# Splitting the first weights of a phase early, taking POOL out of the phase change and fixing ScalarE's order, in a fp32 two-layer decoder trunk on one Trainium2 core

## The chip, the core and the metric

One core of one Trainium2 chip runs the whole program. The engines are TensorE (PE, with its weight loads PEld), VectorE (DVE), ScalarE (ACT), GpSimd (POOL) and SyncE (SP, which here issues nearly all DMAs). The time is device microseconds of one execution; lower is better. Before: 2397.88 us, the median of 3 runs (2392.67 to 2399.52).

## What is computed

A trunk of two layers over 256 tokens and 2048 channels. Layer 0 mixes tokens by a Conformer convolution, layer 1 by differential attention; each is followed by a squared-ReLU MLP of 8192 hidden channels. Scales, shifts and gates come from a condition vector `c` by a product with `ada_w` (six vectors in each layer). Cut to what matters here:

```python
cond = silu(c)
for i in range(2):
    sh_m, sc_m, g_m, sh_f, sc_f, g_f = split(cond @ ada_w[i] + ada_b[i], 6)
    h = x * (1 + sc_m) + sh_m
    y = conformer_conv(h, ...) if i == 0 else diff_attention(h, ...)   # ends in a 2048x2048 projection
    x = layer_norm(alpha * x + g_m * y, ln_mix_g[i], ln_mix_b[i])
    h = x * (1 + sc_f) + sh_f
    y = square(relu(h @ mlp_w1[i] + mlp_b1[i])) @ mlp_w2[i] + mlp_b2[i]
    x = layer_norm(alpha * x + g_f * y, ln_ffn_g[i], ln_ffn_b[i])
```

## The kernel before

**Products.** Every matrix is float32 and is split into a high part (rounded to the fp32r type) and a low part (the rest). A product is the sum of three: high by high, high by low, low by high. `x`-side pairs such as `hT` lie as (channel in chunk, chunk, token); weights stream from DRAM in tiles of 128 x 2048 (four chunks of 128 rows by 512 columns), four raw buffers deep, and are split in halves of 128 x 1024: ACT casts the high half (`wh_...`), DVE or POOL subtracts to get the low half (`wl_...`). There are four buffers for split halves (pool `wsp`). A half serves two chunks, two token halves and three products: 12 products.

**Jobs.** `add_group` cuts a product of 512 output columns into jobs. A normal job is one raw tile, two halves, with both token halves (t = 0, 1) done for each weight half. The last job of a phase (`tail`) and the first of the next (`lead`) hold four halves and run all of them for t = 0 and then for t = 1, so that the layer norm and the next h of t = 0 can be made while t = 1 is multiplied. `run_jobs` writes the program: `fetch(n)` emits load, cast and subtraction of the weight halves up to number n, `half(j, t)` the products, `tick()` releases work that was put off by a number of ticks (a normal job makes two, one for each 12 products). `POOL_LEAD` names the lead halves whose low part POOL makes, `POOL_TAIL` those of the tail.

**Phase change.** There are three: convolution to first MLP (some 485 us into the span), first MLP to attention (1233 us), attention to second MLP (1644 us). At each, the chain for one token half is: gate and add to `z` (L724, L725), statistics (L1152 or L1262, L642, L647), a power on POOL (L120), `nb` (L653), normalise `z` in four quarters, two on ACT (L660) and two on DVE (L662); TensorE transposes four blocks (L453); scale and shift give h (L458 on ACT for blocks 0 and 2, L461 on DVE for blocks 1 and 3), whose high part ACT casts (L411) and whose low part DVE subtracts (L414; POOL for block 3). The scalars for scale and shift come from `h_scalars` (L737 to L740 on DVE). `z` is then multiplied on POOL by the layer norm's gain, for the next residual (`base_x`, L695 to L699, four quarters, each with its own small load on SP), first after 6 ticks, then every 4 or 5.

**Order.** From the first job on, TensorE and DVE run in the order in which the code is written; ACT, POOL and SP run in an order that a scheduler chose when the program was built.

Of the kernel before, what the change touches and what calls it, by code (L numbers as in the profile page):

```python
# [19 lines left out]
P = 128  # L20
# [22 lines left out]
AHEAD = 4  # L43
POOL_LO = (3,)
U_WAIT = 2
POOL_LEAD = (1,2,3)
POOL_TAIL = (-1,-3)
GF_LOAD = 16
M2 = (196, 207)
# [30 lines left out]
def trunk(  # L80
# [431 lines left out]
    def add_group(key, pair, srcs, lead=False, tail=False, pump=None, start=None, pre_t=None, on_t=None,  # L512
                  only=None, prep=None, between=None, on_pool=(), bias=None):
        blocks = [[i] for i in range(len(srcs))]
        if lead:
            blocks[:2] = [[0, 1]]
        if tail:
            blocks[-2:] = [[len(srcs) - 2, len(srcs) - 1]]
        per = srcs[0].shape[1]
        for blk in blocks:  # L520
            if only is not None and blk[0] not in only:
                continue
            first = blk[0] == 0
            jobs.append(dict(key=key, pair=pair, n=2 * len(blk), kc0=blk[0] * per, nk=per * len(srcs),
                             start=start if first else None, pre_t=pre_t if first else None, pre_done=False, prep=prep if first else None, on_t=on_t, bias=bias if first else None,
                             between=between if first else None))
            for i in blk:
                for q in range(2):
                    pool = ((lead and 2 * i + q in POOL_LEAD) or (tail and 2 * (i - len(srcs)) + q in POOL_TAIL)
                            or 2 * i + q in on_pool)  # L530
                    halves.append((f"{key}_{i}", srcs[i], q, pump, nc.gpsimd if pool else nc.vector))

    def fetch(n):
        while len(split) < min(n, len(halves)):
            name, src, q, pump, eng = halves[len(split)]
# [4 lines left out]
            hi = wsp.tile([P, 1024], F32R, tag="whi", name=f"wh_{name}_{q}")  # L540
            lo = wsp.tile([P, 1024], F32R, tag="wlo", name=f"wl_{name}_{q}")
            nc.scalar.copy(hi, rq)  # L542
            eng.tensor_tensor(lo, rq, hi.bitcast(F32), op=ALU.subtract)  # L543
            per = src.shape[1] // 2
            hv = hi.rearrange("p (a n) -> p a n", a=per)
            lv = lo.rearrange("p (a n) -> p a n", a=per)
            split.append([(hv[:, a, :], lv[:, a, :]) for a in range(per)])
            if q == 1 and pump is not None:
                pump()

    def run_jobs():
        banks, h = {}, 0
        for n, job in enumerate(jobs):
            if job["start"] is not None:
                job.pop("start")()
                job["start"] = None
            pair = job["pair"]()
            key, nk = job["key"], job["nk"]
            if job["kc0"] == 0:
                banks[key] = [mm_bank(f"{key}_ps{t}") for t in range(NT)]  # L560
            pss = banks[key]

            def half(j, t):

                steps = []
                kc0 = job["kc0"] + j * len(split[h])
                for a, (wh, wl) in enumerate(split[h + j]):
                    kc = kc0 + a
                    for tt in t:
                        if job["pre_t"] is not None and kc == 0 and (tt or not job["pre_done"]):  # L570
                            for f in job["pre_t"](tt):
                                f()
                        xh = pair[0][:, kc, tt * P:(tt + 1) * P]
                        xl = pair[1][:, kc, tt * P:(tt + 1) * P]
                        if kc == 0 and job["bias"] is not None:
                            for n, (sel, row) in enumerate(job["bias"]()):
                                nc.tensor.matmul(pss[tt], lhsT=sel, rhs=row, start=(n == 0), stop=False)
                        nc.tensor.matmul(pss[tt], lhsT=xh, rhs=wh, start=(kc == 0 and job["bias"] is None),  # L578
                                         stop=False)
                        nc.tensor.matmul(pss[tt], lhsT=xh, rhs=wl, start=False, stop=False)  # L580
                        nc.tensor.matmul(pss[tt], lhsT=xl, rhs=wh, start=False, stop=(kc == nk - 1))  # L581
                        if kc == nk - 1 and job["on_t"] is not None:
                            steps.append(lambda tt=tt: job["on_t"](tt, pss[tt]))
                return steps

            if job["n"] == 2:
                for j in range(2):
                    fetch(h + j + AHEAD)
                    for f in half(j, range(NT)):
                        f()  # L590
                    tick()
            else:
                fetch(h + 4)
                tail = []
                for t in range(NT):
                    if job["between"]:
                        job["between"](GF_USE[2 * t])
                    for j in range(4):
                        if job["between"] and j == 2:
                            job["between"](GF_USE[2 * t + 1])  # L600
                        if t == NT - 1:
                            fetch(h + j + AHEAD)
                        steps = half(j, [t])
                        if steps and t == 0:
                            tail = steps[0]() or []
                            nxt = jobs[n + 1] if n + 1 < len(jobs) else None
                            if nxt is not None and nxt["prep"] is not None:
                                tail.append(nxt["prep"])
# [590 lines left out]
    def mlp(i, ln_g, ln_b, gcol, bcol, pump, at_end, start=None, mid=None):  # L1199
# [32 lines left out]
        for q in range(4):  # L1232
            for g in range(4):
                n0 = q * D + g * NG

                def on_t1(t, ps, q=q, g=g, n0=n0):
# [4 lines left out]
                    def rest():  # L1241
                        pt = tp_tile(f"ut_{i}_{q}_{g}_{t}")
                        for j in range(4):
# [10 lines left out]
                add_group(f"w1_{i}_{q}_{g}", lambda: cur["hT"], wtiles(mlp_w1[i], 0, KC, n0), pump=pump, lead=first,  # L1254
                          start=(lambda q=q: begin_q(q)) if g == 0 else None,
                          pre_t=pre_t if first else None, on_t=on_t1, prep=prep if first else None,
                          between=ada_between if first and i == 0 else None)
            for n in range(4):
                def on_t2(t, ps, q=q, n=n):
# [236 lines left out]
    for g in range(4):  # L1496
        kv = {}
        pair = lambda: sc1["hT"]
        add_group(f"qkv_q{g}", pair, wtiles(attn_qkv_w[0], 0, KC, g * NG), pump=pump_slow, lead=(g == 0),
                  start=begin_attn if g == 0 else None, prep=prep_attn if g == 0 else None, pre_t=pre_attn if g == 0 else None,  # L1500
                  on_t=rope_evac("q", g, kv))
        add_group(f"qkv_k{g}", pair, wtiles(attn_qkv_w[0], 0, KC, D + g * NG), pump=pump_slow,
                  on_t=rope_evac("k", g, kv))
# [80 lines left out]
```

## Time and profile before

| | |
|---|---|
| median of 3 runs | 2397.88 us (2392.67 to 2399.52) |
| the profiled execution's own time | 2392.5 us |
| its span | 2390.7 us, 28609 instructions |
| mean granted clock of TensorE | 0.987 |
| TensorE busy | 95% of the span |
| DVE, ACT, POOL busy | 75%, 44%, 10% |
| DMA | 608.54 MB, mean 255 GB/s |

The profile is of one execution. Times in its rows count from the start of the span. A stage row gives the stretch, its length, then for PE, PEld, DVE, ACT and POOL the busy time and (x) the number of instructions, the clock granted to TensorE as a share of full speed, the mean busy share of the DMA engines and GB/s. Matmuls are pipelined, so their durations overlap; what counts is the distance from one start to the next.

### The profile page before, as it was taken

The page shows a single profiled execution, that of the slowest core. Times are in us where ns is not written, and L with a number is a line of the kernel's source. Part 1 is how long each engine was busy: PE and PEld are TensorE (multiplying, and loading weights), DVE is VectorE, ACT ScalarE, POOL GpSimd, SP SyncE. Part 2 cuts the span into 40 slices and gives each one's busy share as a digit, 9 for nine tenths or more (in the row PEclk, how much of TensorE's full clock was granted, in tenths as well). Part 3 has the DMA queues.
Part 4 walks back from the last instruction along what each step waited for, and adds up shares of the span by engine and source line. Part 5 has one row for each costly group of instructions (what it writes and reads, how often), then busy time and mean ns, then how long its engine had stood idle before and what let it go on. Part 6 is the DMA issues. An engine that isn't in the chain of part 4 may idle for free.

```text
span 2390.7 us, 28609 instructions
## 1 busy us (share of the span) xinstructions
PE 2276.4 (95%) x11167; PEld 1814.2 (76%) x11167; DVE 1802.4 (75%) x2046; ACT 1059.9 (44%) x1360; POOL 247.6 (10%) x162
## 2 busy tenths in 40 slices
PE   5899988999899999999989999998999999999997
PEld 3576646777688888888867888876888888888886
DVE  5887887988888889878868777886876565555566
ACT  3433674254334444434444554544443443443442
POOL 0000001130410000000035001013122000000002
PEclk9999999999999999999999999998999999999998
DMA  9998369969898887888856657684876555556562
GB/s 346 343 321 299 139 250 383 347 206 320 312 321 293 318 317 270 324 313 283 306 185 237 221 185 232 233 316 143 294 263 215 187 193 193 179 192 194 188 219 103
DMA packets 271980, 608.54 MB, mean 255 GB/s; under 512 B 11038, under 2 KB 44388, under 8 KB 258532
## 3 DMA queue, kind: packets, MB, share of 16 engines
q1 hardware_dynamic: 271604, 606.41, 73.2%
q8 instruction: 87, 1.43, 0.2%
q10 hardware_dynamic: 240, 0.30, 0.1%
q14 instruction: 49, 0.40, 0.0%
HBM read 604.54 MB, written 2.13 MB: 254 GB/s over the span
## 4 chain that ended last, share of the span: by engine, by line
PE 78%; DVE 12%; DMA 4%; issue 3%; ACT 2%; POOL 1%; SPq 1%; DVEq 0%; ACTq 0%; POOLq 0%
PE w_ps L578 18%; PE w_ps L581 18%; PE w_ps L580 18%; DVE aacc L249 2%; PE cv L781 2%; PE pw_ps L503 2%; PE pw_ps L504 2%; PE pw_ps L505 2%; DVE wl_w L543 1%; DVE acc L316 1%; PE qkv_q_ps L581 1%; PE qkv_q_ps L580 1%; PE qkv_q_ps L578 1%; PE qkv_v_ps L581 1%; PE qkv_v_ps L578 1%
## 5 line engine op out<-in xcount | busy, mean ns | idle before, releaser
L543 DVE TENSOR_TENSOR wl_w<-w_w,wh_w 128x1024 fp32r<-128x1024 f32 x502 | 634.4, 1282 | 331.4 <-ACT wh_w L542 331.0
L542 ACT CAST wh_w<-w_w 128x1024 fp32r<-128x1024 f32 x512 | 538.3, 1056 | 760.3 <-PE w_ps L581 573.5
L578 PE MATMUL w_ps<-wh_w,hm_hi 128*128 128x512 f32 x1024 | 403.9, 394 | 4.6 <-ACT hm_hi L411 4.6
L580 PE MATMUL w_ps<-wl_w,u_hi 128*128 128x512 f32 x1024 | 398.9, 390 | 6.9 <-DVE wl_w L543 6.9
L580 PE MATMUL w_ps<-wl_w,hm_hi 128*128 128x512 f32 x1024 | 401.0, 392 | 3.8 <-DVE wl_w L543 3.8
L581 PE MATMUL w_ps<-wh_w,hm_lo 128*128 128x512 f32 x1024 | 400.9, 392 | 0.9 <-DVE hm_lo L414 0.9
L578 PE MATMUL w_ps<-wh_w,u_hi 128*128 128x512 f32 x1024 | 400.0, 391 | 0.0
L581 PE MATMUL w_ps<-wh_w,u_lo 128*128 128x512 f32 x1024 | 398.6, 389 | 0.0
L316 DVE SCALAR_TENSOR_TENSOR acc<-adaw,cond,acc 128x2048 f32<-128x2048 f32 (+1 forms) x105 | 245.1, 2334 | 1.1 <-DMA adaw<-in_ada_w_dram 1.0
L578 PEld LDWEIGHTS w_ps<-wh_w,hm_hi 128*128 128x128 f32 x1024 | 193.4, 189 | 48.8 <-ACT hm_hi L411 6.3
L580 PEld LDWEIGHTS w_ps<-wl_w,u_hi 128*128 128x128 f32 x1024 | 192.3, 188 | 48.2 <-DVE wl_w L543 8.9
L580 PEld LDWEIGHTS w_ps<-wl_w,hm_hi 128*128 128x128 f32 x1024 | 193.4, 189 | 44.6 <-DVE wl_w L543 5.5
L581 PEld LDWEIGHTS w_ps<-wh_w,hm_lo 128*128 128x128 f32 x1024 | 193.3, 189 | 43.3 <-DVE hm_lo L414 2.9
L578 PEld LDWEIGHTS w_ps<-wh_w,u_hi 128*128 128x128 f32 x1024 | 192.3, 188 | 42.0 <-issue 1.7
L581 PEld LDWEIGHTS w_ps<-wh_w,u_lo 128*128 128x128 f32 x1024 | 192.3, 188 | 39.8
L543 POOL TENSOR_TENSOR wl_w<-w_w,wh_w 128x1024 fp32r<-128x1024 f32 x10 | 24.0, 2412 | 1099.1 <-ACT wh_w L542 1099.1
L503 PE MATMUL pw_ps<-wh_pw,h_hi 128*128 128x512 f32 x256 | 106.9, 418 | 10.9 <-ACT wh_pw L491 4.1
L504 PE MATMUL pw_ps<-wl_pw,h_hi 128*128 128x512 f32 x256 | 102.6, 401 | 3.6 <-DVE wl_pw L492 3.6
L505 PE MATMUL pw_ps<-wh_pw,h_lo 128*128 128x512 f32 x256 | 102.1, 399 | 0.0
L492 DVE TENSOR_TENSOR wl_pw<-w_pw,wh_pw 128x1024 fp32r<-128x1024 f32 x64 | 77.8, 1221 | 26.1 <-ACT wh_pw L491 25.9
L491 ACT CAST wh_pw<-w_pw 128x1024 fp32r<-128x1024 f32 x64 | 66.0, 1052 | 48.8 <-PE pw_ps L505 37.9
L503 PEld LDWEIGHTS pw_ps<-wh_pw,h_hi 128*128 128x128 f32 x256 | 49.3, 192 | 40.1 <-issue 15.6
(335 smaller groups left out, 3281.6 us busy)
## 6 DMA issues: line engine op xcount, KB each, us to landing
w_w<-in_mlp_w_dram SPq DMA_DIRECT2D x256, 1024.0 KB, 5.3
adaw<-in_ada_w_dram SPq DMA_DIRECT2D x96, 1024.0 KB, 5.8
aw<-in_ada_w_dram SPq DMA_DIRECT2D x49, 1024.0 KB, 8.0
w_pw<-in_conv_pw_w_dram SPq DMA_DIRECT2D x64, 512.0 KB, 9.7
conv_ux<-in_ada_w_dram SPq DMA_DIRECT2D x21, 1024.0 KB, 9.9
w_pw<-in_conv_pw_w_dram SPq DMA_DIRECT2D x16, 1024.0 KB, 7.1
w_qkv_q<-in_attn_qkv_w_dram SPq DMA_DIRECT2D x16, 1024.0 KB, 6.4
w_qkv_k<-in_attn_qkv_w_dram SPq DMA_DIRECT2D x16, 1024.0 KB, 5.2
```

The lines of the kernel that those rows point to most:

```text
L249: nc.vector.scalar_tensor_tensor(st["acc"], wv[:, kc % per, :], cond[:, kc:kc + 1], st["acc"], ALU.mult, ALU.add)
L316: nc.vector.scalar_tensor_tensor(st["acc"], w, cond[:, kc:kc + 1], st["acc"], ALU.mult, ALU.add)
L491: nc.scalar.copy(hq, rq)
L492: nc.vector.tensor_tensor(lq, rq, hq.bitcast(F32), op=ALU.subtract)
L503: nc.tensor.matmul(pss[t], lhsT=xh, rhs=wh, start=(kc == first), stop=False)
L504: nc.tensor.matmul(pss[t], lhsT=xh, rhs=wl, start=False, stop=False)
L505: nc.tensor.matmul(pss[t], lhsT=xl, rhs=wh, start=False, stop=(kc == last))
L542: nc.scalar.copy(hi, rq)
L543: eng.tensor_tensor(lo, rq, hi.bitcast(F32), op=ALU.subtract)
L578: nc.tensor.matmul(pss[tt], lhsT=xh, rhs=wh, start=(kc == 0 and job["bias"] is None), stop=False)
L580: nc.tensor.matmul(pss[tt], lhsT=xh, rhs=wl, start=False, stop=False)
L581: nc.tensor.matmul(pss[tt], lhsT=xl, rhs=wh, start=False, stop=(kc == nk - 1))
```

## The change

Five things are changed together.

1. `lead` becomes a number: so many of the first halves of a phase get buffers of their own (one in the `work` pool under the tag X, a second in the pool `late`, which exists from the first MLP on). Conv to first MLP has 1, the two others 2. They are fetched while the tail job is in its first token half.
2. `POOL_LEAD` is empty: DVE makes all low halves of the lead job. The fourth's low half is put off behind the second token half's normalisation.
3. At attention and the second MLP the scalars of the next h are made at the start of the tail job.
4. ACT joins DVE in the written order from the convolution's output projection to the end.
5. `base_x` starts after 18 ticks in place of 6.

```diff
-POOL_LEAD = (1,2,3)
+POOL_LEAD = ()
...
-    def fetch(n):
+    def fetch(n, low=None):
...
+            if home == "x":
+                hi = work.tile([P, 1024], F32R, tag="X", name=f"wh_{name}_{q}", bufs=3)
+                lo = work.tile([P, 1024], F32R, tag="X", name=f"wl_{name}_{q}", bufs=3)
+            elif home == "late":
+                hi = late["pool"].tile([P, 1024], F32R, tag="whi", name=f"wh_{name}_{q}")
+                lo = late["pool"].tile([P, 1024], F32R, tag="wlo", name=f"wl_{name}_{q}")
...
+                own, more = job["own"], nxt["own"] if nxt is not None else 0
                 fetch(h + 4)
                 tail = []
+                if more and nxt["prep"] is not None and nxt["prep"][0]:
+                    nxt.pop("prep")[1]()
+                    nxt["prep"] = None
                 for t in range(NT):
...
-                        if t == NT - 1:
-                            fetch(h + j + AHEAD)
+                        if t == NT - 1 and not more and not own:
+                            fetch(h + 4 + j)
+                        if t == NT - 1 and more and j >= 2:
+                            fetch(h + 4 + min(more + j - 1, 3))
                         steps = half(j, [t])
+                        if t == 0 and more and 1 <= j <= more:
+                            fetch(h + 4 + j)
+                        if t == NT - 1 and own:
+                            fetch(h + 4 + max(j + 1, own))
...
+                            low = []
                             if feat:
                                 feat.pop(0)()
+                                fetch(h + 4 + 4, low)
                             tail = steps[0]() or []
                             while tail or feat:
                                 if tail:
                                     tail.pop(0)()
+                                flush()
                                 if feat:
                                     feat.pop(0)()
+                                if low and not tail:
+                                    low.pop(0)()
...
-    early_ve = tc.manual_schedule(engines={mybir.EngineType.DVE})
+    early_ve = tc.manual_schedule(engines={mybir.EngineType.DVE, mybir.EngineType.Activation})
...
-            base_x(ln_g, None, f"basem{i}", 6, 4)
+            base_x(ln_g, None, f"basem{i}", 18, 4)
...
-        base_x(ln_ffn_g[0], ln_ffn_b[0], "basea", 6, 5)
+        base_x(ln_ffn_g[0], ln_ffn_b[0], "basea", 18, 5)
```

How that moves instructions: DVE at the change from the first MLP to attention. `w2g` is the gated output of the old group, `lna` the layer norm, `ha` the new h, `wl_qkv_q` the low halves of the new phase's weights; the rows start after the tail's last subtraction. Before:

```order
L724 TENSOR_TENSOR w2g_3_3_0_9394<-w_0_3_3_ps_9296,gbm_4857 128x512
L725 TENSOR_TENSOR z<-z,w2g_3_3_0_9394 128x512
L1262 BN_STATS mlp_st_3109<-z 128x6
L642 BN_AGGR lna_mv<-mlp_st_3109 128x2
L647 TENSOR_SCALAR lna_rs<-lna_mv 128x1
L543 TENSOR_TENSOR wl_qkv_q_0_0_9412<-w_qkv_q_0_9409,wh_qkv_q_0_0_9411 128x1024
L653 SCALAR_TENSOR_TENSOR lna_nb<-lna_mv,lna_rs 128x1
L662 TENSOR_SCALAR z<-z,lna_mv,lna_rs 128x512 x2
L737 TENSOR_SCALAR ha_s_9439<-mod_1_5818 128x16
L738 SCALAR_TENSOR_TENSOR ha_mul<-cols_ln,ha_s_9439 128x16
L739 TENSOR_TENSOR ha_add<-cols_ln,ha_s_9439 128x16
L740 TENSOR_TENSOR ha_add<-ha_add,mod_0_6841 128x16
```

After; the rows start two instructions later after the tail's last subtraction, with `L764` (`ha_s`) and `L765` (`ha_mul`) just ahead of them:

```order
L766 TENSOR_TENSOR ha_add<-cols_ln,ha_s_9372 128x16
L767 TENSOR_TENSOR ha_add<-ha_add,mod_0_6841 128x16
L552 TENSOR_TENSOR wl_qkv_q_0_0_9392<-w_qkv_q_0_9389,wh_qkv_q_0_0_9391 128x1024
L552 TENSOR_TENSOR wl_qkv_q_0_1_9402<-w_qkv_q_0_9389,wh_qkv_q_0_1_9401 128x1024
L751 TENSOR_TENSOR w2g_3_3_0_9411<-w_0_3_3_ps_9296,gbm_4857 128x512
L752 TENSOR_TENSOR z<-z,w2g_3_3_0_9411 128x512
L1289 BN_STATS mlp_st_3109<-z 128x6
L669 BN_AGGR lna_mv<-mlp_st_3109 128x2
L674 TENSOR_SCALAR lna_rs<-lna_mv 128x1
L680 SCALAR_TENSOR_TENSOR lna_nb<-lna_mv,lna_rs 128x1
L689 TENSOR_SCALAR z<-z,lna_mv,lna_rs 128x512 x2
L552 TENSOR_TENSOR wl_qkv_q_1_0_9441<-w_qkv_q_1_9438,wh_qkv_q_1_0_9440 128x1024
```

The four scalar instructions and two subtractions now stand ahead of the old group's statistics, `lna_nb` follows the statistics directly, and a third subtraction stands behind the normalisation, ahead of the second token half's gate.

ACT at the same place, before (`wh_qkv_q` are the weight casts, `lna` on `z` the normalisation, `ha_h` and `ha_hi` h and its high part):

```order
L542 CAST wh_qkv_q_0_0_9411<-w_qkv_q_0_9409 128x1024
L542 CAST wh_qkv_q_0_1_9427<-w_qkv_q_0_9409 128x1024
L542 CAST wh_qkv_q_1_0_9446<-w_qkv_q_1_9444 128x1024
L660 ACTIVATE z<-z,lna_nb,lna_rs 128x512 x2
L542 CAST wh_qkv_q_1_1_9525<-w_qkv_q_1_9444 128x1024
L458 ACTIVATE ha_h_9461<-ha_t_9460,ha_add,ha_mul 128x128 x4
L411 CAST ha_hi<-ha_h_9461 128x4x128
L411 CAST ha_hi<-ha_h_9481 128x4x128
```

After:

```order
L550 CAST wh_qkv_q_0_0_9391<-w_qkv_q_0_9389 128x1024
L550 CAST wh_qkv_q_0_1_9401<-w_qkv_q_0_9389 128x1024
L687 ACTIVATE z<-z,lna_nb,lna_rs 128x512 x2
L550 CAST wh_qkv_q_1_0_9440<-w_qkv_q_1_9438 128x1024
L458 ACTIVATE ha_h_9461<-ha_t_9460,ha_add,ha_mul 128x128 x4
L411 CAST ha_hi<-ha_h_9461 128x4x128
L550 CAST wh_qkv_q_1_1_9471<-w_qkv_q_1_9438 128x1024
L411 CAST ha_hi<-ha_h_9485 128x4x128
```

The normalisation comes ahead of the third cast, which now stands directly between it and h, and the fourth cast stands behind the first block's high part.

POOL at the change from the convolution to the first MLP, before (`lnm_rs` is the power, `basem` the base pass, one pair for each quarter):

```order
L120 TENSOR_TENSOR lnm_rs<-lnm_rs,neg_half 128x1
L543 TENSOR_TENSOR wl_w_0_0_0_0_1_3874<-w_w_0_0_0_0_3845,wh_w_0_0_0_0_1_3873 128x1024
L543 TENSOR_TENSOR wl_w_0_0_0_1_0_3893<-w_w_0_0_0_1_3890,wh_w_0_0_0_1_0_3892 128x1024
L543 TENSOR_TENSOR wl_w_0_0_0_1_1_3972<-w_w_0_0_0_1_3890,wh_w_0_0_0_1_1_3971 128x1024
L120 TENSOR_TENSOR lnm_rs<-lnm_rs,neg_half 128x1
L414 TENSOR_TENSOR hm_lo<-hm_h_3957,hm_hi 128x4x128
L697 TENSOR_TENSOR z<-z,basem_gb_4125 128x512 x2
L414 TENSOR_TENSOR hm_lo<-hm_h_4051,hm_hi 128x4x128
L697 TENSOR_TENSOR z<-z,basem_gb_4230 128x512 x2
L697 TENSOR_TENSOR z<-z,basem_gb_4328 128x512 x2
```

After:

```order
L120 TENSOR_TENSOR lnm_rs<-lnm_rs,neg_half 128x1 x2
L414 TENSOR_TENSOR hm_lo<-hm_h_3962,hm_hi 128x4x128
L414 TENSOR_TENSOR hm_lo<-hm_h_4051,hm_hi 128x4x128
L724 TENSOR_TENSOR z<-z,basem_gb_4403 128x512 x2
L724 TENSOR_TENSOR z<-z,basem_gb_4501 128x512 x2
```

The three subtractions are gone, and the first base pass stands behind both low parts of h.

More of the change, by code (lines that the diff above doesn't have):

```diff
@@ L523, in add_group @@
             first = blk[0] == 0
-            jobs.append(dict(key=key, pair=pair, n=2 * len(blk), kc0=blk[0] * per, nk=per * len(srcs),
+            jobs.append(dict(key=key, pair=pair, n=2 * len(blk), own=int(lead) if first else 0, kc0=blk[0] * per, nk=per * len(srcs),
                              start=start if first else None, pre_t=pre_t if first else None, pre_done=False, prep=prep if first else None, on_t=on_t, bias=bias if first else None,
@@ L530, in add_group @@
                             or 2 * i + q in on_pool)
-                    halves.append((f"{key}_{i}", srcs[i], q, pump, nc.gpsimd if pool else nc.vector))
-    def fetch(n):
+                    home = (None, "x", "late")[2 * i + q + 1] if lead and 2 * i + q < lead else None
+                    halves.append((f"{key}_{i}", srcs[i], q, pump, nc.gpsimd if pool else nc.vector, home))
+    def fetch(n, low=None):
         while len(split) < min(n, len(halves)):
-            name, src, q, pump, eng = halves[len(split)]
+            name, src, q, pump, eng, home = halves[len(split)]
             if q == 0:
@@ L539, in fetch @@
             rq = raws["raw"][:, q * 1024:(q + 1) * 1024]
[L540 to L543, printed above, removed]
+            if home == "x":
[4 more added lines that the diff above has]
+                lo = late["pool"].tile([P, 1024], F32R, tag="wlo", name=f"wl_{name}_{q}")
+            else:
+                hi = wsp.tile([P, 1024], F32R, tag="whi", name=f"wh_{name}_{q}")
+                lo = wsp.tile([P, 1024], F32R, tag="wlo", name=f"wl_{name}_{q}")
+            nc.scalar.copy(hi, rq)
+            if low is None:
+                eng.tensor_tensor(lo, rq, hi.bitcast(F32), op=ALU.subtract)
+            else:
+                low.append(lambda lo=lo, rq=rq, hi=hi, eng=eng: eng.tensor_tensor(
+                    lo, rq, hi.bitcast(F32), op=ALU.subtract))
             per = src.shape[1] // 2
@@ L1253, in mlp @@
                 first = q == 0 and g == 0
-                add_group(f"w1_{i}_{q}_{g}", lambda: cur["hT"], wtiles(mlp_w1[i], 0, KC, n0), pump=pump, lead=first,
+                add_group(f"w1_{i}_{q}_{g}", lambda: cur["hT"], wtiles(mlp_w1[i], 0, KC, n0), pump=pump, lead=(i + 1) * first,
                           start=(lambda q=q: begin_q(q)) if g == 0 else None,
-                          pre_t=pre_t if first else None, on_t=on_t1, prep=prep if first else None,
+                          pre_t=pre_t if first else None, on_t=on_t1, prep=(i == 1, prep) if first else None,
                           between=ada_between if first and i == 0 else None)
@@ L1498, in trunk @@
         pair = lambda: sc1["hT"]
-        add_group(f"qkv_q{g}", pair, wtiles(attn_qkv_w[0], 0, KC, g * NG), pump=pump_slow, lead=(g == 0),
-                  start=begin_attn if g == 0 else None, prep=prep_attn if g == 0 else None, pre_t=pre_attn if g == 0 else None,
+        add_group(f"qkv_q{g}", pair, wtiles(attn_qkv_w[0], 0, KC, g * NG), pump=pump_slow, lead=2 * (g == 0),
+                  start=begin_attn if g == 0 else None, prep=(True, prep_attn) if g == 0 else None, pre_t=pre_attn if g == 0 else None,
                   on_t=rope_evac("q", g, kv))
```

4 lines of the change are left out of this document (2 added, 2 removed).

## The prediction

> **What bounds the kernel now.** I read the page first, then the busy time by stage, then the order of time on each engine around the three phase changes. The page gives the span and TensorE's share; the two stage rows hold, after the stretch and its length, the busy time of PE, PEld, DVE, ACT and POOL, the granted clock, the DMA share and GB/s.
>
> ```profile
> span 2390.7 us, 28609 instructions
> PE 2276.4 (95%) x11167; PEld 1814.2 (76%) x11167; DVE 1802.4 (75%) x2046; ACT 1059.9 (44%) x1360; POOL 247.6 (10%) x162
> 1215.00:1270.00 55.00, 43.31 (x189) 34.08 (x188) 36.91 (x52) 26.38 (x42) 22.31 (x14) 0.91 0.39 129
> 1645.00:1700.00 55.00, 47.17 (x203) 37.76 (x204) 43.30 (x55) 29.71 (x46) 19.21 (x11) 0.88 0.47 163
> ```
>
> TensorE is the bound. Only its idle time, 2390.7 - 2276.4 = 114.3 us, and a clock below full can be won. The change into attention holds 55 - 43.31 = 11.7 us idle at a clock of 0.91, the change into the second MLP 7.8 us at 0.88. TensorE's own order at the change into attention (start, duration, engine and line, what it writes and reads, and in brackets the idle time before it and who ended that):
>
> ```profile
> 1227.54 0.39 PE L578 MATMUL w_ps<-wh_w,u_hi 128*128 128x512 f32 x1
> ...
> 1232.75 0.39 PE L581 MATMUL w_ps<-wh_w,u_lo 128*128 128x512 f32 x1
> ...
> 1243.71 0.79 PE L578 MATMUL qkv_q_ps<-wh_qkv_q,ha_hi 128*128 128x512 f32 x1 [5.28 <-ACT ha_hi L411]
> ...
> 1246.41 0.79 PE L581 MATMUL qkv_q_ps<-wh_qkv_q,ha_lo 128*128 128x512 f32 x1 [1.48 <-DVE ha_lo L414]
> 1247.00 0.63 PE L578 MATMUL qkv_q_ps<-wh_qkv_q,ha_hi 128*128 128x512 f32 x1
> ...
> 1250.84 0.63 PE L578 MATMUL qkv_q_ps<-wh_qkv_q,ha_hi 128*128 128x512 f32 x1
> ...
> 1253.98 1.91 PE L453 MATMUL ha_t<-ident,z 128*128 128x128 f32 x16
> 1256.84 0.50 PE L578 MATMUL qkv_q_ps<-wh_qkv_q,ha_hi 128*128 128x512 f32 x1 [0.94 <-ACT ha_hi L411]
> ```
>
> The last group of the MLP ends at 1232.75 + 0.39 = 1233.1; its second token half was 24 products, 5.21 / 23 = 0.227 us apart. The first product of the new phase starts 10.6 us later, its third (the first to need h's low half) at 1246.41. Then the clock is low: ten products from 1247.00 to 1250.84 are 3.84 / 9 = 0.427 us apart. From 1246.41 to 1253.98 stand 22 products: 7.57 us, where 22 x 0.227 = 5.0 would do, so the clock costs 2.6 us. The weights are not what is waited for: both named waits are for h. Why h is late stands on DVE, POOL and ACT:
>
> ```profile
> 1227.74 0.69 DVE L724 TENSOR_TENSOR w2g<-w_ps,gbm 128x512 f32<-128x512 f32 x1 [5.85 <-PE w_ps L581]
> 1230.22 0.15 DVE L647 TENSOR_SCALAR lna_rs<-lna_mv 128x1 f32<-128x1 f32 x1
> 1230.30 1.23 DVE L543 TENSOR_TENSOR wl_qkv_q<-w_qkv_q,wh_qkv_q 128x1024 fp32r<-128x1024 f32 x1
> 1231.97 2.33 DVE L653 SCALAR_TENSOR_TENSOR lna_nb<-lna_mv,lna_rs 128x1 f32<-128x1 f32 x1 [0.44 <-POOL lna_rs L120]
> 1234.22 3.43 DVE L662 TENSOR_SCALAR z<-z,lna_mv,lna_rs 128x512 f32<-128x512 f32 x2
> 1238.84 2.26 DVE L738 SCALAR_TENSOR_TENSOR ha_mul<-cols_ln,ha_s 128x16 f32<-128x16 f32 x1
> 1246.28 0.15 DVE L653 SCALAR_TENSOR_TENSOR lna_nb<-lna_mv,lna_rs 128x1 f32<-128x1 f32 x1
> 1246.35 0.99 DVE L662 TENSOR_SCALAR z<-z,lna_mv,lna_rs 128x512 f32<-128x512 f32 x2
> 1248.05 1.37 DVE L461 TENSOR_SCALAR ha_h<-ha_t,ha_mul,ha_add 128x128 f32<-128x128 f32 x4
> 1249.33 0.69 DVE L414 TENSOR_TENSOR ha_lo<-ha_h,ha_hi 128x512 fp32r<-128x512 f32 x1
> ```
>
> ```profile
> 1223.43 2.39 POOL L543 TENSOR_TENSOR wl_w<-w_w,wh_w 128x1024 fp32r<-128x1024 f32 x1 [3.05 <-ACT wh_w L542]
> 1230.45 1.48 POOL L120 TENSOR_TENSOR lna_rs<-lna_rs,neg_half 128x1 f32<-128x1 f32 x1 [4.63 <-DVE lna_rs L647]
> 1231.90 2.37 POOL L543 TENSOR_TENSOR wl_qkv_q<-w_qkv_q,wh_qkv_q 128x1024 fp32r<-128x1024 f32 x1
> 1244.02 0.55 POOL L120 TENSOR_TENSOR lna_rs<-lna_rs,neg_half 128x1 f32<-128x1 f32 x1 [2.95 <-DVE lna_rs L647]
> ```
>
> ```profile
> 1234.33 1.52 ACT L660 ACTIVATE z<-z,lna_nb,lna_rs 128x512 f32<-128x512 f32 x2 [1.45 <-DVE lna_nb L653]
> 1241.49 1.51 ACT L458 ACTIVATE ha_h<-ha_t,ha_add,ha_mul 128x128 f32<-128x128 f32 x4 [4.70 <-DVE ha_add L740]
> 1243.03 0.62 ACT L411 CAST ha_hi<-ha_h 128x512 fp32r<-128x512 f32 x1
> ```
>
> The same DVE instruction takes 2.33 us at 1231.97, ending as POOL's subtraction ends (1231.90 + 2.37), and 0.15 us at 1246.28 when POOL has none. So an instruction of one engine holds the other off until it ends. L662 (3.43 against 0.99) and L738, 2.26 us for sixteen columns, stretch in the same way, and ACT waits 4.70 us for h's scalars before its first block. The three low halves on POOL and the base pass put this on the chain of statistics, L653, L662, L737 to L740, ha_h and ha_hi, which is what TensorE waits for.
>
> **The change part by part, at attention.** *No low halves on POOL, scalars early, base pass later.* The blocked excess goes: 2.2 us on L653, 2.4 us on L662, and the four scalar instructions, which now stand ahead of the last group's end, leave the chain (4.70 us of ACT's wait). *Own buffers.* Two halves are cast and subtracted before the statistics. Three subtractions of 1.23 us come to DVE at each phase change, 11 us in all. The new chain, from rows: POOL's subtraction for the old group ends at 1225.8, two DVE subtractions end at 1228.3 (before, L724 started at 1227.74: 0.5 us lost), L724 to L647 take 1230.37 - 1227.74 = 2.63, so 1230.9; power 0.55, so 1231.5 (as low as 0.55 or, held off by DVE, 1.48; DVE has nothing there now, so 0.55); L653 0.15; ACT's L660 1.52, so 1233.2; one weight cast of 1.0 which in written order stands before h, so 1234.2; ha_h 1.51, ha_hi 0.62: first product at 1236.4, before 1243.71. DVE meanwhile does the third subtraction (to 1235.5), L724 to L647 for the second token half (1238.1) and the low half (0.69): third product at 1238.8, before 1246.41, so 7.6 us. Then 22 products at full clock, 5.0, and about 0.5 for the second block's low half (1238.8 + 1.37 + 0.15 + 0.99 + 0.69 = 1242.0, wanted after twelve products at 1241.5): 1244.3, before 1253.98.
>
> Part of this is given back. ACT must finish all four blocks of the first token half before the first of the second, and two of them wait for DVE. The second block's cast ends at 1240.8 (1238.8 + 1.37 + 0.62), L660 1242.3, ha_h 1243.8, ha_hi 1244.5; DVE's low half and ha_h (0.69, 1.37) 1246.5; ha_hi 1247.2; ha_h and ha_hi of the second token half 1249.3. Its first product starts there, with 3 us of TensorE idle, before 1256.84. **Gain 7.5 us.** The nine added subtractions are hidden behind products except the two named delays.
>
> **The second MLP** has the same code:
>
> ```profile
> 1643.25 0.39 PE L581 MATMUL wo_ps<-wh_wo,attno_lo 128*128 128x512 f32 x1
> ...
> 1666.42 0.50 PE L578 MATMUL w_ps<-wh_w,hm_hi 128*128 128x512 f32 x1 [0.94 <-ACT hm_hi L411]
> ...
> 1673.17 0.50 PE L580 MATMUL w_ps<-wl_w,hm_hi 128*128 128x512 f32 x1 [0.52 <-DVE wl_w L543]
> ```
>
> From 1643.6 to 1666.42 are 22.8 us; the chain above needs 1249.3 - 1233.1 = 16.2. With the 0.52 us wait, which comes while POOL's base pass holds DVE, **gain 7.1 us**. Here and at attention the bounds are 4.5 (the clock stays low, 2.6 less) and 10 (the 3 us of second-half idle not there).
>
> **The first MLP** keeps its scalars late.
>
> ```profile
> 481.23 2.35 DVE L653 SCALAR_TENSOR_TENSOR lnm_nb<-lnm_mv,lnm_rs 128x1 f32<-128x1 f32 x1 [0.43 <-POOL lnm_rs L120]
> ...
> 517.78 4.73 POOL L697 TENSOR_TENSOR z<-z,basem_gb 128x512 f32<-128x512 f32 x2 [11.39 <-DMA basem_gb<-in_ln_mix_g_dram]
> 519.04 4.55 DVE L543 TENSOR_TENSOR wl_w<-w_w,wh_w 128x1024 fp32r<-128x1024 f32 x2
> ...
> 558.04 0.50 PE L580 MATMUL w_ps<-wl_w,hm_hi 128*128 128x512 f32 x1 [3.24 <-DVE wl_w L543]
> ```
>
> Gone are the 2.2 us of hold on L653; two subtractions (2.46) now stand between it and the second half's statistics, and the second half's chain absorbs the rest. Bounds 0 and 2.2; I take 0.8. *Base pass.* While POOL's L697 ran, two subtractions took 4.55 instead of 2.46: 2.1 us of hold for one quarter. Three quarters there delay the weights that stall TensorE 3.24 us at 558. They move twelve ticks later, of 12 products x 0.227 = 2.7 us each, and their loads on SP stand behind later weight loads. Bounds: 3.2 won, or 3.2 lost where the hold now lands; I take 1.5 won, because right after the phase change DVE has the least in hand. In the other two phases it goes under products at no cost.
>
> *ACT in written order* I cost at nothing: with four buffers a cast starts three halves, 3 x 2.7 = 8.2 us, ahead of its products, which covers the cast (1.0), the subtraction (1.23) and a wait of some 6 us. If that cover goes, see the second rival.
>
> **Sum:** 7.5 + 7.1 + 0.8 + 1.5 = 16.9 us. The profiled execution took 2392.5 us (span 2390.7), 5.4 below the median of 2397.88; taken from the median, 2381.0 us.
>
> **Rivals.** *The clock stays low.* My chain leaves TensorE gaps of about 1.3 and 2 us with two products between them, and 3 us later on. A gap of 2.46 us kept full clock in the first MLP (0.40 against 0.63 after a gap of 5.28):
>
> ```profile
> 488.48 0.66 PE L453 MATMUL hm_t<-ident,z 128*128 128x128 f32 x4 [2.46 <-ACT hm_h L458]
> ...
> 491.26 0.40 PE L580 MATMUL w_ps<-wl_w,hm_hi 128*128 128x512 f32 x1
> ```
>
> If it falls at both changes, 5.2 us go: 2386.2; with the base pass costing 3.2 instead of winning 1.5, 9.9 go: 2390.9, no change. The Trainium skill (TensorE: Matmul & The Clock Gate, Part 1) has the clock halved after an idle window of about 3.4 us, free-running; by that rule all my gaps keep it unless the window counts the share of work in it, and the sum is 2381.0 by the first reading and 2386.2 by the second; the trace agrees for 2.46 and 5.28.
>
> *ACT in written order blocks the weight casts (slower).* In both MLPs two weight casts now stand behind both casts of u, which wait for DVE:
>
> ```profile
> 551.83 2.01 ACT L542 CAST wh_w<-w_w 128x1024 fp32r<-128x1024 f32 x2 [5.20 <-DMA w_w<-in_mlp_w_dram]
> ...
> 555.51 0.62 ACT L411 CAST u_hi<-r 128x512 fp32r<-128x512 f32 x1 [0.70 <-DVE r L1250]
> ```
>
> Here they would start at 556.1, 4.3 us later. Sixteen groups in the first MLP; if TensorE lost 1.06 us in each, the gain is gone, and at 1.5 us the time is 2381.0 + 24 = 2405. Against it: their low halves on DVE stand behind u's low halves before and after, so these move by about 0.5 us only.
>
> *The halves were the wait.* If the own buffers alone mattered, nothing would be won, since no wait of the new phase's first products names them; then 2398.
>
> **Chances.** Forecast, 12 to 24 us won: 0.60, its own range 2374 to 2386. Clock low or base pass costly, 7.2 to 12 won: 0.19. Both, or the halves: within 0.3% (7.2 us, about what a measurement can tell here): 0.15. ACT blocks: 0.06. So faster 0.79, same 0.15, slower 0.06; range 2371 to 2391.
>
> **What would show it.** At attention, L653 near 0.15 us, no POOL subtraction between the statistics and h, first product about 3.3 us after the old group's end instead of 10.6, products 0.227 us apart at once; the second half's wait for ha_hi grown from 0.94 to about 3. The stall at 558 gone or moved. Wrong if waits for weight halves grow in the MLPs, or if L724 waits long behind the two early subtractions.

## Result: 32 us slower, though the phase changes gained what was forecast

The changed kernel takes 2427.65 us (median of 5 runs, 2422.18 to 2431.42), against 2395.26 us for the kernel before in its runs: a ratio of 1.0132, with a 95% interval of 1.0121 to 1.0143. The forecast was 2381 us, with a range of 2371 to 2391. The page of after:

```profile
span 2425.9 us, 28592 instructions
PE 2291.7 (94%) x11167; PEld 1822.5 (75%) x11167; DVE 1797.3 (74%) x2055; ACT 1050.3 (43%) x1360; POOL 212.4 (9%) x153
```

All engines do about the same work; TensorE's idle time grew from 114.3 to 2425.9 - 2291.7 = 134.2 us, and it worked 15 us longer for the same products, so part of the loss is a low clock: the mean granted clock was 0.982, before 0.987. TensorE at the change into attention (start, duration, engine, line, and in brackets the idle time before and who ended it):

```profile
1246.18 0.39 PE L593 MATMUL w_ps<-wh_w,u_lo 128*128 128x512 f32 x1
...
1249.46 0.50 PE L590 MATMUL qkv_q_ps<-wh_qkv_q,ha_hi 128*128 128x512 f32 x1 [1.14 <-ACT ha_hi L411]
...
1251.80 0.50 PE L593 MATMUL qkv_q_ps<-wh_qkv_q,ha_lo 128*128 128x512 f32 x1 [1.61 <-DVE ha_lo L414]
1252.13 0.53 PE L590 MATMUL qkv_q_ps<-wh_qkv_q,ha_hi 128*128 128x512 f32 x1
...
1255.45 0.49 PE L593 MATMUL qkv_q_ps<-wh_qkv_q,ha_lo 128*128 128x512 f32 x1
...
1258.53 1.91 PE L453 MATMUL ha_t<-ident,z 128*128 128x128 f32 x16
1261.93 0.50 PE L590 MATMUL qkv_q_ps<-wh_qkv_q,ha_hi 128*128 128x512 f32 x1 [1.49 <-ACT ha_hi L411]
```

The first product comes 2.9 us after the old group's end at 1246.57 (before 10.6), and the second token half starts 15.4 us after it (before 23.7). DVE and POOL at the same place:

```profile
1243.87 0.15 DVE L674 TENSOR_SCALAR lna_rs<-lna_mv 128x1 f32<-128x1 f32 x1
1244.68 0.16 DVE L680 SCALAR_TENSOR_TENSOR lna_nb<-lna_mv,lna_rs 128x1 f32<-128x1 f32 x1 [0.66 <-POOL lna_rs L120]
1244.76 1.00 DVE L689 TENSOR_SCALAR z<-z,lna_mv,lna_rs 128x512 f32<-128x512 f32 x2
```

```profile
1244.10 0.55 POOL L120 TENSOR_TENSOR lna_rs<-lna_rs,neg_half 128x1 f32<-128x1 f32 x1 [4.83 <-DVE lna_rs L674]
```

The two held instructions, 2.33 and 3.43 us before, take 0.16 and 1.00, the power 0.55 instead of 1.48. Where the time went is seen from TensorE's order, which is the same in all kernels: the start of the same product in two traces gives what was lost or won up to there. In us against the profiled execution of before (positive is lost), by stage, with four kernels of the experiments:

| stage | after | before, ACT written | after, ACT free | also base pass at 6 | also bias pass late |
|---|---|---|---|---|---|
| up to the end of the convolution | +5.1 | +1.3 | +2.1 | +2.1 | +1.6 |
| change into the first MLP | -1.0 | +5.7 | -2.5 | -2.5 | -2.5 |
| first MLP, from its first group on | +9.3 | +7.0 | +4.6 | 0.0 | -5.8 |
| change into attention, to the first K product | -8.8 | -1.6 | -8.1 | -8.5 | -11.0 |
| attention and its output projection | +36.0 | +35.2 | -0.6 | 0.0 | +1.5 |
| change into the second MLP | -7.5 | -2.7 | -9.7 | -9.4 | -9.5 |
| second MLP | +1.6 | +0.5 | +0.9 | 0.0 | +0.7 |
| sum | +34.7 | +45.4 | -13.3 | -18.2 | -25.1 |

The first row varies between runs of equal code; 3.1 of after's 5.1 us are products at a low clock between 375 and 382 us, which the other kernel in written order does not have. The phase changes won 17 us; attention lost 36.

**What happens in attention.** TensorE's two costliest waits in after, and the same two in before, behind them (who waited, for whom, us in total, times, longest):

```profile
PE at_a L1487 <- DVE at_sm L1480: 12.5, 4, 7.0
PE qkt_k L1441 <- DVE rp_k L1436: 10.3, 7, 2.7
```

```profile
PE qkt_k L1414 <- DVE rp_k L1409: 1.2, 1, 1.2
PE at_a L1460 <- DVE at_sm L1453: 0.5, 1, 0.5
```

Of the 36.0 us, 23.0 are idle time of TensorE; the other 13.0 are the same products taking longer, at a granted clock of 0.97 over the stretch where before it was 1.00. TensorE waits for DVE (the softmax `at_sm`, the rotated K `rp_k`), and DVE is late because of ACT. ACT's waits there for DVE and POOL, in before and in after:

```profile
ACT at_on L1478 <- POOL at_ss L120: 27.0, 13, 3.9
ACT at_sm L1444 <- DVE at_mx L1441: 9.9, 15, 1.4
ACT attno_hi L411 <- DVE at_o L1489: 2.4, 3, 1.3
```

```profile
ACT attno_hi L411 <- DVE at_o L1516: 72.6, 16, 8.4
ACT at_sm L1471 <- DVE at_mx L1468: 56.7, 16, 8.2
ACT at_on L1505 <- POOL at_ss L120: 25.3, 16, 3.6
```

Before, 12 us of waiting for DVE; after, 129. One place, first in after: ACT (the exponentials L1471, casts L550, the unit's output L411), then DVE, then TensorE.

```profile
1349.41 1.07 ACT L550 CAST wh_qkv_k<-w_qkv_k 128x1024 fp32r<-128x1024 f32 x1
1358.65 0.51 ACT L1471 ACTIVATE at_sm<-at_sm,at_mx 128x256 f32<-128x256 f32 x1 [8.18 <-DVE at_mx L1468]
...
1359.66 1.03 ACT L550 CAST wh_qkv_k<-w_qkv_k 128x1024 fp32r<-128x1024 f32 x1
1364.77 0.41 ACT L411 CAST attno_hi<-at_o 128x256 fp32r<-128x256 f32 x1 [4.07 <-DVE at_o L1516]
```

```profile
1358.45 0.17 DVE L1468 TENSOR_SCALAR at_mx<-at_mx 128x2 f32<-128x2 f32 x1
1360.73 1.22 DVE L552 TENSOR_TENSOR wl_qkv_k<-w_qkv_k,wh_qkv_k 128x1024 fp32r<-128x1024 f32 x1 [2.11 <-ACT wh_qkv_k L550]
1361.87 2.35 DVE L316 SCALAR_TENSOR_TENSOR acc<-adaw,cond,acc 128x2048 f32<-128x2048 f32 x1
...
1365.29 0.48 DVE L1480 SCALAR_TENSOR_TENSOR at_sm<-at_sm,at_rz 128x256 f32<-128x256 f32 x1
```

```profile
1365.83 0.69 PE L1487 MATMUL at_a<-ident,at_sm 128*128 128x128 f32 x2 [3.32 <-DVE at_sm L1480]
```

The same place before, on ACT and DVE:

```profile
1351.17 1.05 ACT L542 CAST wh_qkv_k<-w_qkv_k 128x1024 fp32r<-128x1024 f32 x1 [2.59 <-PE qkv_k_ps L581]
1352.52 0.51 ACT L1444 ACTIVATE at_sm<-at_sm,at_mx 128x256 f32<-128x256 f32 x1 [0.30 <-DVE at_mx L1441]
```

```profile
1352.31 0.17 DVE L1441 TENSOR_SCALAR at_mx<-at_mx 128x2 f32<-128x2 f32 x1
1352.39 1.22 DVE L543 TENSOR_TENSOR wl_qkv_k<-w_qkv_k,wh_qkv_k 128x1024 fp32r<-128x1024 f32 x1
```

Before, the scheduler put the cast ahead of the exponentials, so DVE finds it done as soon as it has the maxima. In written order the cast stands behind the exponentials, these wait 8.18 us for DVE's maxima, and DVE's next instruction is the subtraction that waits for the cast, with the softmax's own next steps behind it. Each engine in turn waits for the other, and TensorE idles 3.32 us. The Trainium skill (PSUM — Partial Sum Buffer, "Engine vs sequencer instructions") states that the queues of these engines are strictly first in, first out; the trace agrees: nothing passed the exponentials in those 8.18 us.

### The profile page after: what moved, and what is told of

Read it like the earlier page. It is cut to its first block, busy times and chain, and to the rows that moved or that the text cites. A ratio compares the mean times of both kernels' runs of the same rounds, so it can differ in the third digit from the quotient of the medians.

```text
span 2425.9 us, 28592 instructions
## 1 busy us (share of the span) xinstructions
PE 2291.7 (94%) x11167; PEld 1822.5 (75%) x11167; DVE 1797.3 (74%) x2055; ACT 1050.3 (43%) x1360; POOL 212.4 (9%) x153
## 4 chain that ended last, share of the span: by engine, by line
PE 71%; DVE 16%; ACT 4%; DMA 4%; issue 3%; POOL 1%; SPq 1%; DVEq 0%; ACTq 0%; POOLq 0%
PE w_ps L593 17%; PE w_ps L590 17%; PE w_ps L592 17%; DVE acc L316 2%; DVE wl_w L552 2%; DVE aacc L249 2%; PE cv L808 2%; PE pw_ps L503 2%; PE pw_ps L504 2%; PE pw_ps L505 1%; PE ut L1271 1%; PE aps L290 1%; DVE wl_pw L492 1%; PE qkv_q_ps L593 1%; PE qkv_v_ps L590 1%
## 5 line engine op out<-in xcount | busy, mean ns | idle before, releaser
L550 ACT CAST wh_w<-w_w 128x1024 fp32r<-128x1024 f32 x512 | 533.9, 1054 | 620.2 <-PE w_ps L593 505.6
L552 POOL TENSOR_TENSOR wl_w<-w_w,wh_w 128x1024 fp32r<-128x1024 f32 x4 | 9.6, 2396 | 1102.4 <-ACT wh_w L550 1102.4
L411 ACT CAST u_hi<-r 128x512 fp32r<-128x512 f32 x64 | 39.9, 624 | 146.6 <-DVE r L1277 146.6
```

## Experiments

**ACT back in the scheduler's order**, all else as in after:

```diff
-    early_ve = tc.manual_schedule(engines={mybir.EngineType.DVE, mybir.EngineType.Activation})
+    early_ve = tc.manual_schedule(engines={mybir.EngineType.DVE})
```

> The changed kernel with ACT taken out of the written order again (the scheduler's order, as before); the other four parts stay. In the trace after, 36 us are lost between the first products of K and the last of the output projection of attention, 8 us in the first MLP, while the three phase changes gain 17. Theory W (ACT's written order makes these losses: an instruction that waits for DVE or a DMA stands ahead of weight casts and of copies that TensorE needs): all of the 36 and most of the 8 return; of the 17, up to 2 us at each of two changes are lost, since four weight casts then stand ahead of h on ACT: 2380 to 2390 us. Theory B (the later base pass makes them: POOL's products now hold DVE inside attention and the first MLP, and a cascade starts there): ACT's order is irrelevant, 2418 to 2428 us.

Measured: 2379.55 us (2378.54 to 2380.82), ratio to before 0.9939 (0.9925 to 0.9952). Theory W holds, and the time is 0.45 us below its range: 48.1 us come back, and attention is at -0.6.

**The opposite edit on the kernel before: only ACT in written order.**

> The kernel before with one edit: ACT in written order. Theory W: the losses of the changed kernel without its gains: 2395 plus 36 to 45, 2431 to 2440 us, with waits of TensorE for at_sm and rp_k in attention that the kernel before does not have. Theory B: 2390 to 2400 us.

Measured: 2441.54 us (2438.40 to 2447.15), ratio 1.0200 (1.0185 to 1.0215): 47.5 us, the same price without the other four parts; attention +35.2. The time is 1.5 us above theory W's range.

**Base pass back at 6 ticks in the changed kernel** (`basem` and `basea`, 18 to 6).

> The changed kernel with the base pass back at 6 ticks. Theory W: the losses in attention stay (30 us or more); the first MLP wins or loses a few us: 2420 to 2430 us. Theory B: the losses go, the gains of the phase changes stay less some 4 us for the hold after them: 2382 to 2390 us.

Measured: 2425.39 us (2422.69 to 2429.03), ratio 1.0129 (1.0113 to 1.0144). Attention still loses 35.2 us, so theory B falls.

**ACT in written order only around the phase changes** (the context is entered at the tail job and left after the lead job):

```diff
+                if more:
+                    act_order = tc.manual_schedule(engines={mybir.EngineType.Activation})
+                    act_order.__enter__()
...
+                if own:
+                    act_order.__exit__(None, None, None)
```

> The changed kernel with ACT in written order only from the start of a phase's tail job to the end of the next phase's lead job, and in the scheduler's order elsewhere. Theory W: the phase changes gain as in the trace after (8.8, 7.5 and 1 us) and the losses are gone: 2378 us, 2374 to 2384. Theory B: the losses stay, 2418 to 2428 us. If instead both orders lose in attention because of what the phase change leaves behind (all work some 9 us nearer together), 2390 to 2410.

Measured: 2385.28 us (2381.99 to 2385.66), ratio 0.9959 (0.9947 to 0.9972). Attention's loss is gone (+0.4 in its trace), but the time is 1.3 us above theory W's range and 5.7 us above that with ACT free throughout: the written order does not help at the phase changes either. The changes into the first and the second MLP cost 3.1 and 2.2 us more than in the scheduler's order, so the casts that stand ahead of h in that order, which I had priced at up to 2 us each, were no loss.

**Written order in attention alone** (ACT free elsewhere).

> The kernel with ACT free (2379.6 us) with one stretch in written order: ACT from the end of attention's lead job to the start of the tail job of the output projection. Theory W by place: the 36 us lie in attention itself and come back with this stretch alone: 2411 to 2419 us. Rival (they need what the written order leaves behind in the first MLP, or the window at the phase change): under 2400 us.

Measured: 2414.32 us (2412.78 to 2416.20), ratio 1.0081 (1.0066 to 1.0096): 34.8 us more than with ACT free. Its trace loses 37.1 us against before between the first K product and the last of the output projection. The loss lies there and needs nothing from elsewhere.

**Which instructions block: the waiting ones one tick later, in the changed kernel.** The exponentials and the second pass over a unit's output become steps of their own, emitted behind the next weight cast:

```diff
-        return s1, s1b, s2, s3, s4
+        return s1, s1x, s1b, s2, s3, s3x, s4
...
-    plan = {False: ((4, 8, 12, 16), (5, 9, 13, 17), (7, 11, 15, 19), (10, 14, 18, 22), (13, 17, 21, 25)),
+    plan = {False: ((4, 8, 12, 16), (5, 9, 13, 17), (6, 10, 14, 18), (7, 11, 15, 19), (10, 14, 18, 22), (11, 15, 19, 23), (13, 17, 21, 25)),
...
```

> The changed kernel (ACT in written order, 2427.7 us) with the two ACT instructions of each attention unit that wait longest, the exponentials and the second pass over the output (L1471, L1505), written one tick later, behind the next weight cast; the reciprocal of the sums moves one tick later with them. Theory H (head of the line: those waiting instructions keep the casts behind them from starting): the 36 us lost in attention fall to 18 or less, 2392 to 2410 us. Rival L (any fixed order of ACT against DVE's fixed order loses there, whichever instruction waits): 2420 to 2432 us.

Measured: 2409.84 us, with three runs of 2398.39 to 2402.33 and six of 2409.22 to 2412.24; ratio 1.0055 (1.0039 to 1.0071). By the median 17.8 us come back, just within theory H. The profiled execution is one of the three (2399.54 us); in it attention loses 13.6 us where after loses 36.0 (the 5 us that the next expectation gives for it are not what the stage shows). What sets the two levels apart stays open. ACT's waits in attention in that execution say what is left:

```profile
ACT attno_hi L411 <- DVE at_o L1524: 72.8, 16, 9.2
ACT at_sm L1475 <- DVE at_mx L1468: 6.8, 8, 1.3
```

The third waiting instruction then went one tick later too (the cast and subtraction of a unit's output become `s4x`).

> The kernel with the exponentials and the second pass over the output one tick later (2409.8 us), and the third waiting instruction as well: the cast of the unit's output (L411 on attno_hi), which in that run still waits 72.8 us for DVE in attention, goes one tick later, behind the next weight cast. Theory H (head of the line): the rest of the loss in attention, 5 us in its profiled execution and 18 by the medians, goes as well: 2390 to 2400 us. Rival L (the rest comes from the fixed order as such): 2405 to 2412 us.

```profile
ACT at_sm L1475 <- DVE at_mx L1468: 24.5, 16, 5.8
ACT attno_hi L411 <- DVE at_o L1524: 16.4, 9, 2.8
```

Measured: 2395.52 us (2391.20 to 2399.76), ratio 0.9998 (0.9989 to 1.0008). With ACT still in written order, 32.1 us of the time are back, attention loses 3.0 us instead of 36.0, and these waits for DVE fall from 129 to 41 us. Theory H holds for attention: it was the place of three instructions that wait, not a fixed order as such. The kernel is still 16.0 us slower than with ACT free; by the two traces 4.5 of them lie in the first MLP, 3.6 in attention and 3.6 at the change into the second MLP.

**The base pass with ACT free.**

> The kernel with ACT free (2379.6 us) and the base pass back at 6 ticks. Theory P1: the later pass wins at the changes into attention (1.5 us) and the second MLP (3.9 us), as the runs in written order show, but loses 3 us in the first MLP, where it now holds DVE at 577 to 592 us and a new wait of 1.9 us stands at 583 us: 2381 to 2384 us, with that wait gone. Rival P2 (the prediction: the later pass wins in the first MLP as well): 2385 to 2389 us.

Measured: 2373.76 us (2372.89 to 2375.01), ratio 0.9912 (0.9897 to 0.9927): 5.8 us won by going back to 6, where both theories expected a loss. The later pass wins nothing at the changes (-8.1 and -9.7 with it, -8.5 and -9.4 without) and costs 4.6 us in the first MLP. TensorE there with the pass late, and with it early:

```profile
556.51 0.50 PE L592 MATMUL w_ps<-wl_w,hm_hi 128*128 128x512 f32 x1 [2.79 <-DVE wl_w L552]
583.02 0.50 PE L592 MATMUL w_ps<-wl_w,hm_hi 128*128 128x512 f32 x1 [1.91 <-DVE wl_w L552]
```

```profile
557.45 0.63 PE L592 MATMUL w_ps<-wl_w,hm_hi 128*128 128x512 f32 x1 [3.22 <-DVE wl_w L552]
```

The stall at about 557 us stands in both, so the pass is not its cause, though the prediction took it to be; the one at 583 us is new.

**The first MLP's bias pass on POOL put off**, base pass there at 6, ACT free:

```diff
-            base_x(ln_g, None, f"basem{i}", 18, 4)
+            base_x(ln_g, None, f"basem{i}", 18 if i else 6, 4)
...
+                defer(44, lambda: base_bias(gate["gb"], mlp_b2[i], f"basem{i}", 20, ln_b))
```

> The kernel with ACT free, the base pass of the first MLP back at 6 ticks (the others stay at 18), and the first MLP's bias pass on POOL (L737 to L745) put off by 44 ticks, a quarter every 20. Theory P1 with hold (POOL's passes are what stretches DVE at 605 to 680 us, where TensorE waits some 5 us for low halves): 3 us from the base pass and 4 to 6 from the bias pass: 2370 to 2374 us. Rival D (DVE is full there with its own work, and the bias pass only costs where it stands): 2375 to 2379 us.

Measured: 2367.38 us (2363.75 to 2368.91), ratio 0.9883 (0.9867 to 0.9899): the fastest of all, 28 us below before in its own runs and 2.6 us below the range of theory P1. The stretch of the first MLP from the transposes of its first group to those of its fifth (and the four groups of the second matrix between them), with the bias pass where it was and put off (columns as in the prediction's stage rows):

```profile
521.60:716.60 195.00, 183.29 (x812) 148.39 (x811) 170.20 (x135) 75.31 (x82) 48.00 (x24) 0.99 0.90 317
```

```profile
521.10:708.50 187.40, 182.96 (x813) 149.69 (x812) 156.29 (x135) 75.90 (x82) 8.58 (x4) 0.98 0.89 319
```

DVE runs 135 instructions in both and needs 13.9 us less for them once POOL's bias pass is gone; TensorE's waits for low halves between 600 and 690 us (6.8 us) go, and the stretch is 7.6 us shorter.

**The parts that gained, one after the other, on the kernel before.** First `POOL_LEAD = ()` alone:

> The kernel before with one edit: no low halves of a lead job on POOL. Theory H (POOL's subtraction holds DVE's L653 and L662 for 4.6 us at the change into attention, likewise at the two others): the hold goes, but three subtractions of 1.23 us come to the same chain: 1 to 2 us won at each change, 2388 to 2392 us. Rival N (without buffers of their own the halves cost on DVE what the hold did): 2393 to 2398 us.

Measured: 2390.64 us (2388.98 to 2393.50), ratio 0.9979 (0.9970 to 0.9988): 4.9 us. The sum is theory H's, the places are not: 1.3 us are lost at the change into the first MLP and 1.1 in it, 3.3 won at attention and 3.7 at the second MLP.

Then the scalars of h at the start of the tail job as well:

> The kernel before without low halves on POOL for a lead job (2390.6 us) and with the scalars of h made at the start of the tail job at attention and the second MLP. Theory S (the scalars stand on the chain ahead of h; ACT waited 4.7 us for them at attention): 2 to 4 us more won at each of the two changes, 2383 to 2387 us. Rival O (two subtractions still stand between the statistics and h, so that only buffers of their own for the first halves free the chain): 2388 to 2392 us.

Measured: 2385.74 us (2383.55 to 2388.18), ratio 0.9961 (0.9946 to 0.9976): 9.9 us in all, so 5.0 for the scalars, and the time is in theory S's range. The places do not bear the theory out: between the two traces 1.9 us are won at attention and 0.3 at the second MLP, and the rest of the difference lies ahead of both, where the scalars were not moved. What early scalars are worth on their own is thus some 2 us by the traces. The own buffers, with the fourth low half put off, are the rest to the kernel with ACT free and the pass at 6: 21.8 - 9.9 = 11.9 us. That is a difference between runs; the buffers were not tried alone. Its places fit: 5.4, 3.3 and 5.4 us at the three changes.

## Why the prediction was wrong, step by step

- **No low halves on POOL, scalars early, own buffers: right as a whole.** At attention the first product was forecast 3.3 us after the old group's end and the second token half 16.2; measured 2.9 and 15.4. The gains were forecast at 7.5 and 7.1 us, measured 8.8 and 7.5 in the trace of after, and 8.5 and 9.4 with ACT free and the base pass at 6. Of the given-back wait, forecast at 3 us, 1.49 came.
- **Low clock: in part.** After the waits of 1.14 and 1.61 us eight steps take 3.32 us, 1252.13 to 1255.45, where 8 x 0.227 = 1.82 would do: 1.5 of the 2.6 us stayed, less than the rival's case. The Trainium skill (TensorE: Matmul & The Clock Gate, Part 1) has the clock halved after an idle window of about 3.4 us. Here shorter gaps with work between them sufficed, and the traces bear out the prediction's second reading, by which the share of work counts (rows in the last section).
- **The first MLP: 0.8 us forecast, 1.0 measured in after**, 2.5 with ACT free, just above the upper bound of 2.2.
- **Base pass: 1.5 us won forecast, 5.8 lost measured** with ACT free, beyond the bound of 3.2. The term rested on blaming the stall at 558 us on the pass; it stands with the pass at either place. How the later pass costs its 4.6 us in the first MLP, by holding DVE or by its loads, was not separated.
- **ACT in written order, costed at nothing: the step that failed.** It costs 48 us, 36 of them in attention. The cover (four buffers, some 6 us of wait) was worked out for the MLP's groups alone, and the slower rival too was priced there, at sixteen times 1.5 us and a chance of 0.06. The order inside attention was never read, although 16 units stand there with three ACT instructions each that wait for DVE or POOL. In the first MLP the rival's mechanism does occur: ACT's casts of u wait 78.2 us for DVE (32 waits), before 13.8 (18 waits). But it costs TensorE little, since DVE's subtractions stand behind u's low halves in either order, as the prediction argued. The 4.7 us that the written order costs there come mainly at two places, which the prediction did not name (below).
- Without that step the sum was near: with ACT free the other four parts give 2379.55 us against 2381.0, where the base pass' 5.8 us lost were made up by gains of 21.8 where 15.4 were forecast. Two errors cancelled there, so the nearness is in part luck.

The two places in the first MLP, in after. At the first, ACT's copy `us` stands behind a cast that waits for its weights' DMA. At the second, a cast stands behind a sine that waits for DVE; DVE's next subtraction waits 1.27 us for that cast, u comes later by it, and the casts behind u's casts are what TensorE waits for. ACT, then TensorE:

```profile
603.07 1.05 ACT L550 CAST wh_w<-w_w 128x1024 fp32r<-128x1024 f32 x1 [7.23 <-DMA w_w<-in_mlp_w_dram]
604.02 1.07 ACT L1265 COPY us<-w_ps 128x512 f32<-128x512 f32 x2
...
933.86 0.26 ACT L1359 ACTIVATE rope<-rr_0.25_7141 128x64 f32<-128x64 f32 x1 [4.50 <-DVE rr_0.25_7141 L1358]
934.02 1.04 ACT L550 CAST wh_w<-w_w 128x1024 fp32r<-128x1024 f32 x1
937.68 0.63 ACT L411 CAST u_hi<-r 128x512 fp32r<-128x512 f32 x1 [2.62 <-DVE r L1277]
...
939.53 2.94 ACT L550 CAST wh_w<-w_w 128x1024 fp32r<-128x1024 f32 x3
```

```profile
604.65 1.14 PE L1271 MATMUL ut<-ident,us 128*128 128x128 f32 x8 [2.79 <-ACT us L1265]
...
940.62 0.50 PE L590 MATMUL w_ps<-wh_w,hm_hi 128*128 128x512 f32 x1 [1.34 <-ACT wh_w L550]
```

In before the scheduler had put the copy, at 592.61, ahead of the cast, at 596.38.

## What to carry to other kernels

A change of an engine's order has to be read in every stage that it spans, above all where that engine's instructions wait for another engine that also runs in a fixed order: two fixed orders take turns, and what an instruction blocks is everything behind it. If an order must be fixed, put work that others need (here weight casts) ahead of the instructions that wait; moving three of them by a tick took the loss in attention from 36.0 to 3.0 us. And price the moved work by the stage it lands in: a pass on an idle engine is not free where it holds a busy one.

## What was not expected of the hardware

The hold between POOL and DVE adds up: with 48.0 against 8.6 us of POOL's passes in a stretch of the first MLP, the same 135 DVE instructions took 170.20 against 156.29 us. Twelve of them account for most of it, each some 1.1 us longer (a subtraction 2.30 instead of 1.22), and all but five of the others took what they take without the passes. The Trainium skill (SBUF — State Buffer, "SBUF: two separate sides") states that DVE and GpSimd share a port pair which, when a DVE instruction runs in a two-port mode or reads two inputs from SBUF, one of them holds for a whole instruction; the rows agree in kind.

And the clock fell after gaps of 1.14 and 1.61 us with two products between them, while the single gap of 2.46 us in the kernel before kept it. In these traces the granted clock changes on a grid of 3.41 us. The stretch of that grid ahead of the low clock in after and the low one itself, and the two stretches of before that the gap of 2.46 us falls into (columns as in the stage rows):

```profile
1248.83:1252.24 3.41, 1.18 (x4) 0.70 (x5) 3.27 (x8) 1.53 (x2) 0.93 (x1) 1.00 0.00 0
1252.24:1255.65 3.41, 3.41 (x10) 2.64 (x9) 3.41 (x8) 2.60 (x5) 0.00 (x0) 0.50 0.00 0
```

```profile
483.61:487.02 3.41, 2.17 (x15) 1.48 (x13) 3.27 (x10) 3.41 (x5) 0.86 (x1) 1.00 0.74 212
487.02:490.43 3.41, 1.95 (x20) 0.84 (x20) 3.21 (x8) 2.58 (x7) 3.41 (x2) 1.00 0.31 119
```

TensorE was busy for 1.18 of 3.41 us in the first, and for 2.17 and 1.95 in the last two, so the length of a gap did not decide, but the busy share of a stretch. The thirteen traces say the same from 400 to 2360 us: of the stretches at full clock, all 83 in which TensorE was busy for less than 0.43 of the time were followed by half the clock, none of 7176 above 0.6 was, and between the two 16 of 78 were.
